# Modulation products in a two-block transformer kernel: held behind weight products in three feed-forwards, begun earlier in the last mixer

## The chip, the cores and the metric

One core of one Trainium2 chip. The metric is the device time of one execution in microseconds, given as the median of three runs.

## The reference

Everything is float32, 256 tokens of width 1024. Block 1 has two layers (mixer, layer norm, a relu-squared feed-forward, a per-layer gate). Block 2 has two layers, each of this form (`mod_c`, `hc` are the same for a context stream of 256 tokens):

```
mod = (silu(c) @ w_mod[i] + b_mod[i])              # 1024 x 6144 weights
sh1, sc1, g1, sh2, sc2, g2 = split(mod, 6)          # parts j = 0 .. 5
h = rms_norm(x, norm_mix[i]) * (1 + sc1) + sh1
y = concat([gla, neighbourhood_attention + na bias, sliding_window_attention]) @ w_out[i]   # inputs: h @ w_in[i]
x = x + g1 * y
h = rms_norm(x, norm_ffn[i]) * (1 + sc2) + sh2
x = x + g2 * ((silu(h @ w_gate[i]) * (h @ w_up[i])) @ w_down[i])
```

Parts 3 and 4 (sh2, sc2) are needed at the start of a layer's feed-forward, part 5 (g2) only at its end. They depend on `c` alone, so they can be computed at any time before.

## The kernel before

**Weight products.** All products with large weights go through one stream (`WeightStream`, L201 on). Each unit of up to 512 KB is loaded by SP into a tile `wr` (4 buffers), cast by ScalarE to its high part `wh` (L214) and split by VectorE into its low part `wl` (L216); TensorE then runs three matmuls per tile and column group (high by high, low by high, high by low), for instance L279 to L281 in the mixers and L1473 to L1475 in the last feed-forwards' gate and up products. DMA issues stand in SP's queue in one order; an issue that waits for a free buffer holds all that follow it.

**Modulations.** `modulation(l, box, js)` (L938) gives four pieces per part j. A piece loads two 512 KB tiles of w_mod (L955) and runs eight matmuls (L957), which the trace shows as 16 records, into a PSUM tile `fil`; VectorE adds the sum to `bm` or `gate` (L959), and after the fourth piece some small work makes the scale and shift `mf`. The w_mod tiles use the tag `fr`, which has 2 buffers. The neighbourhood attention of block 2's layers loads its bias (L1214, one tile for each of three head pairs) into the same two buffers.

**Order.** The kernel's text makes lists of pieces, puts them together with `weave(a, b)` (spreads b evenly over a) and runs them in that order; a scheduler in the framework then places the instructions of each engine by its own estimate of times, so that a piece of the list may move ahead of what stands before it. On the chip each engine works its own queue in that order.

**Last layer's mixer** (block 2 layer 1). 16 pieces of dense input products come first, then further dense pieces and the gated linear attention (GLA, L1053 to L1160 on TensorE). They form `rest` (L1450); the attention pieces (scores L1229, maxima L1239 and L1242, which reads the bias, exponentials L1249, products with values L1285) are woven between. `side["swa"]` holds here the modulations of parts 3 and 4 (eight pieces), woven into the pieces from the sixteenth on. Then comes the output projection (L279 to L281), and between it and the feed-forward the norm with its transposes (L177, tile `sc`, from `a`, L996), the high and low split (L378, L379) and the sums of squares. I call this stretch the seam.

**Feed-forwards with modulations woven in.** Block 1 layer 1 has part 4 of layer 0; block 2 layer 0 has part 2 of layer 1; the last feed-forward has part 5 of layer 1 (four pieces).

## Time and profile before

| | us |
|---|---|
| median of three runs (lowest, highest) | 1923.53 (1917.25, 1923.91) |
| the profiled execution | 1920.0 |
| its span | 1918.2 |
| TensorE busy in it | 1842.1 (96%) |

The span runs from the first to the last instruction that the profiler shows; the profiled execution's own time is 1.8 us longer. Engines: PE is TensorE, DVE is VectorE, ACT is ScalarE, POOL is GpSimd, SP issues DMAs. "L957" is a line of the kernel before. In a timeline row the bracket gives how long the engine sat idle before it, and what it waited for. A clock of 1.00 is 2.4 GHz, and the lower level is 1.2 GHz; a window's figure is the mean over it. Starts of rows that follow each other closely tell TensorE's pace; the length of a single matmul includes its way through the array.

### The profile page before, as it was taken

The numbers are of one execution on the slowest core, as the hardware profiler recorded it, in microseconds if no ns is written. First come the engines' busy times: TensorE is split into PE (matmuls) and PEld (weight loads), VectorE is DVE, ScalarE is ACT, GpSimd is POOL, SyncE is SP. The second block draws the span as 40 slices with busy tenths as digits, with TensorE's granted clock in tenths as the row PEclk, the third lists the DMA queues.
The fourth block names the chain that finished last, engine by engine and source line by source line (L and its number), as shares of the span: only waits on it lengthen the run. The fifth ranks groups of instructions, "written<-read, shape, count | busy, mean of one in ns | idle before, by whom it ended". The sixth has DMA issues, their size and how long they took to land. (4 is left out here: it accounts for less than half of the span.)

```text
span 1918.2 us, 31907 instructions
## 1 busy us (share of the span) xinstructions
PE 1842.1 (96%) x12481; PEld 1574.4 (82%) x12481; DVE 1224.2 (64%) x2333; ACT 988.7 (52%) x1630; POOL 51.0 (3%) x74
## 2 busy tenths in 40 slices
PE   7999999999999899999899999999999999989997
PEld 5766888997887688888787889899898886669997
DVE  5565656656666666668577876685646666755545
ACT  5463564554565364544568553454546556344443
POOL 1000000000000000000000000000000000000000
PEclk9999999999999899999899999999999999989999
DMA  8746654545756554465353355556665464456652
GB/s 282 253 162 212 217 184 144 176 154 192 220 167 198 191 189 151 169 219 174 118 170 103 122 163 167 168 182 192 195 212 168 153 187 146 140 177 187 184 181 98
DMA packets 100835, 338.84 MB, mean 177 GB/s; under 512 B 11572, under 2 KB 12812, under 8 KB 100684
## 3 DMA queue, kind: packets, MB, share of 16 engines
q1 hardware_dynamic: 100140, 336.43, 54.3%
q8 instruction: 98, 1.61, 0.3%
q0 software_dynamic: 544, 0.36, 0.2%
q14 instruction: 53, 0.43, 0.1%
HBM read 335.70 MB, written 1.05 MB: 176 GB/s over the span
## 5 line engine op out<-in xcount | busy, mean ns | idle before, releaser
L216 DVE TENSOR_TENSOR wl<-wr,wh 128x1024 fp32r<-128x1024 f32 (+3 forms) x562 | 638.0, 1137 | 412.6 <-ACT wh L214 406.0
L214 ACT CAST wh<-wr 128x1024 fp32r<-128x1024 f32 (+3 forms) x562 | 549.6, 981 | 655.5 <-PE acc L281 134.6
L279 PE MATMUL acc<-wh,mh 128*128 128x256 f32 (+3 forms) x400 | 132.0, 336 | 3.5 <-ACT mh L378 2.0
L280 PE MATMUL acc<-wl,mh 128*128 128x256 f32 (+3 forms) x400 | 130.8, 329 | 0.7 <-DVE wl L216 0.7
L281 PE MATMUL acc<-wh,ml 128*128 128x256 f32 (+3 forms) x400 | 131.1, 330 | 0.0
L279 PE MATMUL acc<-wh,xh 128*128 128x512 f32 (+3 forms) x304 | 117.0, 394 | 6.1 <-ACT xh L378 3.8
L280 PE MATMUL acc<-wl,xh 128*128 128x512 f32 (+3 forms) x304 | 117.9, 388 | 2.5 <-DVE wl L216 2.5
L281 PE MATMUL acc<-wh,xl 128*128 128x512 f32 (+3 forms) x304 | 117.4, 387 | 0.1
L850 PE MATMUL acc<-wh,a 128*128 128x512 f32 x256 | 102.4, 403 | 0.0
L851 PE MATMUL acc<-wl,a 128*128 128x512 f32 x256 | 101.9, 398 | 0.0
L852 PE MATMUL acc<-wh,a 128*128 128x512 f32 x256 | 101.6, 398 | 0.0
L1473 PE MATMUL sc<-xh,wh 128*128 128x256 f32 x352 | 99.7, 284 | 0.0
L1474 PE MATMUL sc<-xl,wh 128*128 128x256 f32 x352 | 99.5, 283 | 0.0
L1475 PE MATMUL sc<-xh,wl 128*128 128x256 f32 x352 | 99.5, 283 | 0.0
L1474 PE MATMUL sc<-ml,wh 128*128 128x256 f32 x352 | 99.1, 282 | 0.0
L1473 PE MATMUL sc<-mh,wh 128*128 128x256 f32 x352 | 98.9, 281 | 0.0
L1475 PE MATMUL sc<-mh,wl 128*128 128x256 f32 x352 | 98.4, 279 | 0.0
L279 PEld LDWEIGHTS acc<-wh,mh 128*128 128x128 f32 x400 | 75.2, 189 | 14.1 <-issue 3.2
L280 PEld LDWEIGHTS acc<-wl,mh 128*128 128x128 f32 x400 | 75.7, 189 | 6.6 <-DVE wl L216 1.3
L281 PEld LDWEIGHTS acc<-wh,ml 128*128 128x128 f32 x400 | 75.6, 189 | 6.7 <-issue 0.6
L279 PEld LDWEIGHTS acc<-wh,xh 128*128 128x128 f32 x304 | 58.1, 193 | 22.8 <-ACT wh L214 4.6
L825 PE MATMUL sc<-mh,wh 128*128 128x256 f32 x256 | 74.6, 293 | 1.6 <-DVE ml L358 1.6
(570 smaller groups left out, 4683.4 us busy)
## 6 DMA issues: line engine op xcount, KB each, us to landing
wr<-in_ffn_w_dram SPq DMA_DIRECT2D x128, 512.0 KB
fr<-in_w_mod_dram SPq DMA_DIRECT2D x90, 512.0 KB
wr<-in_w_gate_dram SPq DMA_DIRECT2D x66, 512.0 KB
wr<-in_w_up_dram SPq DMA_DIRECT2D x66, 512.0 KB
wr<-in_w_down_dram SPq DMA_DIRECT2D x66, 512.0 KB
wr<-in_w_in_dram SPq DMA_DIRECT2D x40, 384.0 KB
wr<-in_ev_w_in_dram SPq DMA_DIRECT2D x28, 512.0 KB
wr<-in_w_in_dram SPq DMA_DIRECT2D x28, 512.0 KB
```

The source lines that it names most:

```text
L214: S.copy(hi, raw)
L216: V.tensor_tensor(lo, raw, hi, ALU.subtract)
L279: mm(o, xh[:, k, :], wh[:, kk, :], start=(u == 0 and kk == 0), stop=False)
L280: mm(o, xh[:, k, :], wl[:, kk, :], start=False, stop=False)
L281: mm(o, xl[:, k, :], wh[:, kk, :], start=False, stop=(u == nu - 1 and kk == 1))
L825: mm(o, wh[:, kk, bs], mh, start=(k == 0 and b % 2 == 0), stop=False, skip_group_check=True)
L850: mm(o, hh[:, b, ts_], wh[:, kk, :], start=(b == 0), stop=False)
L851: mm(o, hh[:, b, ts_], wl[:, kk, :], start=False, stop=False)
L852: mm(o, hl[:, b, ts_], wh[:, kk, :], start=False, stop=(b == 3))
L1473: mm(o, wh[:, kk, bs], mh, start=(k == 0 and b == 0), stop=False, skip_group_check=True)
L1474: mm(o, wh[:, kk, bs], ml, start=False, stop=False, skip_group_check=True)
L1475: mm(o, wl[:, kk, bs], mh, start=False, stop=(k == 7), skip_group_check=True)
```

## The change

Every third matmul of a weight product goes through a wrapper that remembers it as `dense[0]`. `modulation` takes `hold`; where it is set, a piece's eight matmuls are told to stand behind the last weight product that had been written when the piece was. It is set for the three feed-forwards' modulations. In the last mixer the first four of the eight pieces of parts 3 and 4 are woven into the first 16 dense pieces, and the other four into the rest.

```diff
+    dense = []
+    def wm(*args, **kw):
+        dense[:] = [mm(*args, **kw).ins]
...
-                mm(o, xl[:, k, :], wh[:, kk, :], start=False, stop=(u == nu - 1 and kk == 1))
+                wm(o, xl[:, k, :], wh[:, kk, :], start=False, stop=(u == nu - 1 and kk == 1))
...
-    def modulation(l, box, js):
+    def modulation(l, box, js, hold):
...
-                for g in range(4):
-                    mm(ps[32 * g:32 * g + 32, 0:256], cT[:, k, :], raw[:, 256 * g:256 * g + 256],
-                       start=(k == 2 * u), stop=(k == 2 * u + 1), tile_position=(0, 32 * g))
+                with (tc.issue_after(dense[0]) if hold else nullcontext()):
+                    for g in range(4):
+                        mm(ps[32 * g:32 * g + 32, 0:256], cT[:, k, :], raw[:, 256 * g:256 * g + 256],
+                           start=(k == 2 * u), stop=(k == 2 * u + 1), tile_position=(0, 32 * g))
...
-            rest = dense[:16] + weave(dense[16:] + g, side["swa"])
+            rest = weave(dense[:16], side["swa"][:4]) + weave(dense[16:] + g, side["swa"][4:])
...
-                                                        ffn=weave(ctx_b[:-2], mod(0, 4)), end=flat(ctx_b[-2:]), last=[]))
+                                                        ffn=weave(ctx_b[:-2], mod(0, 4, hold=True)), end=flat(ctx_b[-2:]), last=[]))
...
-        "na": ffn_n, "swa": ffn_c, "pre": [], "from": 2, "ffn": weave([do(layer2_params, 1, prs[1])] + G(["norm", "kv", "znv", "gla"]), mod(1, 2)), "end": L(["nk", "skv"])})
+        "na": ffn_n, "swa": ffn_c, "pre": [], "from": 2, "ffn": weave([do(layer2_params, 1, prs[1])] + G(["norm", "kv", "znv", "gla"]), mod(1, 2, hold=True)), "end": L(["nk", "skv"])})
...
-        "swa": mod(1, 3, 4), "from": 2, "ffn": mod(1, 5), "end": [],
+        "swa": mod(1, 3, 4), "from": 2, "ffn": mod(1, 5, hold=True), "end": [],
```

The instructions move in three places only. In block 1 layer 1's feed-forward one group of four modulation matmuls moves back by 24 rows of TensorE's queue; in block 2 layer 0's nothing moves. The other two places are below; lines from L938 on stand 7 or 8 further down in the changed kernel, and the third matmul of a weight product has the wrapper's line, L157.

TensorE's queue before, where the last mixer's attention and dense products meet: `sc` are scores of one pair of heads and one half of the tokens, `sm` and `acc` its transposed weights, `acc` of L1285 its product with the values, `wh` and `wl` weights.

```order
L1229 MATMUL sc_16127<-a_3091_15894,a_3076_15793 128x256
...
L1229 MATMUL sc_16241<-a_3091_15894,a_3076_15793 128x256
...
L177 MATMUL sm_16147<-ident_61,t_3133_16041 128x128 x4
L177 MATMUL acc_16153<-ident_61,t_3134_16042 128x128 x4
L1285 MATMUL acc_16159<-t_3135_16053,a_3056_15657 64x128
...
L177 MATMUL sm_16261<-ident_61,t_3155_16133 128x128 x4
L279 MATMUL acc_16225<-wh_16069,mh_15310 128x512
L280 MATMUL acc_16225<-wl_16071,mh_15310 128x512
L281 MATMUL acc_16225<-wh_16069,ml_15311 128x512
```

The same place now, up to the same weight products (L286, L287; here `acc_16302`), with the modulation's `fil`:

```order
L1237 MATMUL sc_16127<-a_3091_15894,a_3076_15793 128x256
...
L965 MATMUL fil_16071<-fr_16072,cT_72 32x256 x4
L965 MATMUL fil_16071<-fr_16078,cT_72 32x256 x4
L184 MATMUL sm_16147<-ident_61,t_3133_16041 128x128 x4
L184 MATMUL acc_16153<-ident_61,t_3134_16042 128x128 x4
...
L1237 MATMUL sc_16239<-a_3091_15894,a_3076_15793 128x256
...
L1237 MATMUL sc_16338<-a_3091_15894,a_3076_15793 128x256
...
L184 MATMUL sm_16259<-ident_61,t_3156_16133 128x128 x4
L184 MATMUL acc_16265<-ident_61,t_3157_16134 128x128 x4
L1293 MATMUL acc_16271<-t_3158_16145,a_3056_15657 64x128
...
L286 MATMUL acc_16302<-wh_16087,mh_15310 128x512
```

The dense products now stand behind a piece of modulation, another pair's scores (`sc_16338`) and the whole of the second attention set (`sm_16259` to L1293).

SP's queue before, at the same place; `na_bias` loads are those that the attention's L1242 (now L1250) reads.

```order
L1214 DMA fr_15939<-in_na_bias_dram 128x1024
L1214 DMA fr_16123<-in_na_bias_dram 128x1024
L212 DMA wr_15260<-in_w_in_dram 128x768
...
L212 DMA wr_16284<-in_w_in_dram 128x1024
L1214 DMA fr_16345<-in_na_bias_dram 128x1024
L212 DMA wr_16302<-in_w_in_dram 128x1024
L212 DMA wr_16320<-in_w_in_dram 128x1024
L955 DMA fr_16585<-in_w_mod_dram 128x1024
```

And now:

```order
L1222 DMA fr_15939<-in_na_bias_dram 128x1024
L962 DMA fr_16072<-in_w_mod_dram 128x1024
L219 DMA wr_15260<-in_w_in_dram 128x768
...
L219 DMA wr_16316<-in_w_in_dram 128x1024
L962 DMA fr_16078<-in_w_mod_dram 128x1024
L219 DMA wr_16381<-in_w_in_dram 128x1024
L1222 DMA fr_16123<-in_na_bias_dram 128x1024
L219 DMA wr_16399<-in_w_in_dram 128x1024
L962 DMA fr_16283<-in_w_mod_dram 128x1024
L962 DMA fr_16289<-in_w_mod_dram 128x1024
L1222 DMA fr_16334<-in_na_bias_dram 128x1024
L962 DMA fr_16470<-in_w_mod_dram 128x1024
```

The second pair's bias (`fr_16123`) stood right behind the first pair's before; now a w_mod load has that place, and the bias is issued behind a second w_mod load and a weight load. The third pair's (`fr_16345` before, `fr_16334` now) is issued behind two more w_mod loads.

TensorE's queue in the seam before, between the last output products and the feed-forward; `fil` are pieces of part 5, `sc` the norm's transposes.

```order
L281 MATMUL acc_17389<-wh_17275,c_3095_15900 128x512
L957 MATMUL fil_17918<-fr_17919,cT_72 32x256 x4
L957 MATMUL fil_17918<-fr_17925,cT_72 32x256 x4
L177 MATMUL sc_17365<-ident_61,a_3432_17362 128x128 x4
L177 MATMUL sc_17377<-ident_61,a_3432_17362 128x128 x4
L957 MATMUL fil_18262<-fr_18263,cT_72 32x256 x4
L957 MATMUL fil_18262<-fr_18269,cT_72 32x256 x4
L177 MATMUL sc_17427<-ident_61,a_3442_17424 128x128 x4
L957 MATMUL fil_18606<-fr_18607,cT_72 32x256 x4
L177 MATMUL sc_17439<-ident_61,a_3442_17424 128x128 x4
L957 MATMUL fil_18606<-fr_18613,cT_72 32x256 x4
```

And now:

```order
L157 MATMUL acc_17389<-wh_17275,c_3095_15900 128x512
L184 MATMUL sc_17365<-ident_61,a_3432_17362 128x128 x4
L184 MATMUL sc_17377<-ident_61,a_3432_17362 128x128 x4
L184 MATMUL sc_17427<-ident_61,a_3442_17424 128x128 x4
L184 MATMUL sc_17439<-ident_61,a_3442_17424 128x128 x4
L1481 MATMUL sc_17457<-xh_17185,wh_17305 128x256
L1481 MATMUL sc_17458<-xh_17185,wh_17317 128x256
L1482 MATMUL sc_17457<-xl_17186,wh_17305 128x256
```

Four pieces of part 5 stand now inside the feed-forward, each in one block of eight matmuls; before, three stood in the seam, and the fourth in the feed-forward in two parts, of one and of seven matmuls.

## Rows read from the trace of the kernel before

**Rows 1.** The page, busy time of TensorE: us, share of the span, instructions

```profile
PE 1842.1 (96%) x12481; PEld 1574.4 (82%) x12481; DVE 1224.2 (64%) x2333; ACT 988.7 (52%) x1630; POOL 51.0 (3%) x74
```

**Rows 2.** Windows: start:end, length, busy of each engine, TensorE's clock, DMA share, GB/s

```profile
1632.00:1640.00 8.00, 8.00 (x58) 5.67 (x58) 7.12 (x27) 1.98 (x8) 1.03 (x2) 0.64 0.05 8
1640.00:1672.00 32.00, 27.57 (x319) 19.98 (x316) 24.66 (x91) 12.03 (x39) 1.95 (x3) 1.00 0.56 181
1728.00:1776.00 48.00, 48.00 (x351) 45.57 (x350) 25.63 (x25) 21.94 (x25) 0.00 (x0) 1.00 0.63 190
```

**Rows 3.** Timeline of TensorE, last mixer's start: start, us, operation, [idle before <-releaser]

```profile
1574.80 0.60 PE L1229 MATMUL sc<-ck,a 64*128 64x256 f32 x4
...
1579.39 0.76 PE L177 MATMUL sm<-ident,t 128*128 128x128 f32 x4
...
1582.84 0.81 PE L177 MATMUL sm<-ident,t 128*128 128x128 f32 x4
1583.41 0.48 PE L279 MATMUL acc<-wh,mh 128*128 128x512 f32 x1
```

**Rows 4.** Timeline of SP's DMA issues, last mixer's start

```profile
1573.50 0.40 SPq L1214 DMA_DIRECT2D fr<-in_na_bias_dram  x1
1574.64 2.72 SPq L212 DMA_DIRECT2D wr<-in_w_in_dram  x2
```

**Rows 5.** Timeline of VectorE, last mixer's start

```profile
1576.92 0.48 DVE L1242 CUSTOM_DVE_ANT_0 t<-sc,fr,mx 128x256 f32<-128x256 f32 x1
```

**Rows 6.** Chain of waits, GLA phase: start, length, what

```profile
1659.05 3.82 DMA fr<-in_w_mod_dram
```

**Rows 7.** Chain of waits, seam between last mixer and last feed-forward

```profile
1702.31 6.26 DMA fr<-in_w_mod_dram
```

**Rows 8.** Timeline of TensorE, GLA phase

```profile
1626.39 1.07 PE L957 MATMUL fil<-fr,cT 128*32 128x256 f32 x16 [1.48 <-DVE bm L959]
...
1663.01 0.64 PE L957 MATMUL fil<-fr,cT 128*32 128x256 f32 x8 [3.00 <-DMA fr<-in_w_mod_dram]
```

**Rows 9.** Timeline of TensorE, the seam

```profile
1701.17 1.07 PE L957 MATMUL fil<-fr,cT 128*32 128x256 f32 x16
1704.92 1.09 PE L177 MATMUL sc<-ident,a 128*128 128x128 f32 x8 [2.67 <-DVE a L996]
...
1708.61 1.08 PE L957 MATMUL fil<-fr,cT 128*32 128x256 f32 x8 [1.06 <-DMA fr<-in_w_mod_dram]
1712.29 1.09 PE L177 MATMUL sc<-ident,a 128*128 128x128 f32 x4 [2.59 <-DVE a L996]
...
1716.38 0.38 PE L1473 MATMUL sc<-xh,wh 128*128 128x256 f32 x1
1716.60 0.28 PE L1474 MATMUL sc<-xl,wh 128*128 128x256 f32 x1
1716.71 0.28 PE L1475 MATMUL sc<-xh,wl 128*128 128x256 f32 x1
...
1719.43 0.62 PE L957 MATMUL fil<-fr,cT 128*32 128x256 f32 x2
```

**Rows 10.** Timeline of VectorE, the seam

```profile
1709.76 0.43 DVE L959 TENSOR_TENSOR gate<-fil,gate 128x256 f32<-128x256 f32 x1 [0.74 <-PE fil L957]
```

**Rows 11.** Timeline of TensorE, start of block 1 layer 1's feed-forward

```profile
662.23 0.58 PE L825 MATMUL sc<-mh,wh 128*128 128x256 f32 x1 [1.64 <-DVE ml L358]
662.61 0.41 PE L826 MATMUL sc<-ml,wh 128*128 128x256 f32 x1
662.83 0.41 PE L827 MATMUL sc<-mh,wl 128*128 128x256 f32 x1
...
668.53 0.28 PE L825 MATMUL sc<-mh,wh 128*128 128x256 f32 x1
668.65 0.28 PE L826 MATMUL sc<-ml,wh 128*128 128x256 f32 x1
```

**Rows 12.** Timeline of TensorE, inside the last feed-forward

```profile
1865.57 1.06 PE L957 MATMUL fil<-fr,cT 128*32 128x256 f32 x14
```

More of the change, by code (lines that the diff above doesn't have):

```diff
@@ L1 @@
 import math
+from contextlib import nullcontext
 from contextlib import ExitStack
@@ L326, in part @@
                     mm(o, wh[:, kk, bs], ml, start=False, stop=False, skip_group_check=True)
-                    mm(o, wl[:, kk, bs], mh, start=False, stop=(k == kdim - 1), skip_group_check=True)
+                    wm(o, wl[:, kk, bs], mh, start=False, stop=(k == kdim - 1), skip_group_check=True)
             if 2 * u == kdim - 2:
@@ L826, in up_part @@
                     mm(o, wh[:, kk, bs], ml, start=False, stop=False, skip_group_check=True)
-                    mm(o, wl[:, kk, bs], mh, start=False, stop=(k == 7), skip_group_check=True)
+                    wm(o, wl[:, kk, bs], mh, start=False, stop=(k == 7), skip_group_check=True)
             if u == 3:
@@ L851, in down_part @@
                             mm(o, hh[:, b, ts_], wl[:, kk, :], start=False, stop=False)
-                            mm(o, hl[:, b, ts_], wh[:, kk, :], start=False, stop=(b == 3))
+                            wm(o, hl[:, b, ts_], wh[:, kk, :], start=False, stop=(b == 3))
                     if 1 in hs:
@@ L1474, in up_part @@
                     mm(o, wh[:, kk, bs], ml, start=False, stop=False, skip_group_check=True)
-                    mm(o, wl[:, kk, bs], mh, start=False, stop=(k == 7), skip_group_check=True)
+                    wm(o, wl[:, kk, bs], mh, start=False, stop=(k == 7), skip_group_check=True)
             if m == 1 and u == 1:
@@ L1500, in down_part @@
                             mm(o, hh[:, kk, ts_], wl[:, kk, :], start=False, stop=False)
-                            mm(o, hl[:, kk, ts_], wh[:, kk, :], start=False, stop=(kk == 1 and g == NG - 1))
+                            wm(o, hl[:, kk, ts_], wh[:, kk, :], start=False, stop=(kk == 1 and g == NG - 1))
                     if NG - 1 in gs:
@@ L1553, in up_part @@
                     mm(o, wh[:, kk, bs], ml, start=False, stop=False, skip_group_check=True)
-                    mm(o, wl[:, kk, bs], mh, start=False, stop=(k == 7), skip_group_check=True)
+                    wm(o, wl[:, kk, bs], mh, start=False, stop=(k == 7), skip_group_check=True)
             if u == 0:
@@ L1579, in down_part @@
                         mm(o, h[:, 0, kk, ts_], wl[:, kk, :], start=False, stop=False)
-                        mm(o, h[:, 1, kk, ts_], wh[:, kk, :], start=False, stop=(kk == 1))
+                        wm(o, h[:, 1, kk, ts_], wh[:, kk, :], start=False, stop=(kk == 1))
                     if g == 0:
@@ L1661, in body, with mod @@
     program = [do(begin)]
-    def mod(l, *js):
-        return modulation(l, boxes[l], js)
+    def mod(l, *js, hold=False):
+        return modulation(l, boxes[l], js, hold)
     program += block1_layer(0, xTs[0], to_next(1), dict(tail=flat(ctx_a[:1]), lr=4, mix=mod(0, 0, 1) + ctx_n + mod(0, 2), first=flat(ctx_a[1:2]) + mod(0, 3),
```

## The prediction

> **What bounds the kernel now.** I began with the page: TensorE is busy 96% of the span [rows 1], so the time is its work, plus the stretches where it idles or runs at the low clock. The windows say where those are. In the last feed-forward it has no idle time at all, 48.00 of 48.00 us at full clock [rows 2]: what is put in there costs its whole length. In the last mixer's GLA phase it idles, 4.43 of the 32 us from 1640, and from 1632 to 1640 it works all the time but at a mean clock of 0.64 [rows 2]: VectorE's and ScalarE's chain decides there, and work put between is partly free. The timeline of the seam gives waits of 2.67, 1.06 and 2.59 us, 6.32 in all [rows 9], and the chain of waits passes there through a load of w_mod that took 6.26 us from issue to landing, a piece of the modulation and VectorE's L959 [rows 7, 9, 10]. No modulation matmul disappears: the change moves pieces between these three kinds of stretch.
>
> **The two early holds.** In block 1 layer 1's feed-forward one block of four matmuls goes back by 24 rows, among weight products, and in block 2 layer 0's nothing moves. TensorE meets the same work in both; the bound from both sides is one block's length, half of the 1.07 us that 16 records take [rows 8], and I take 0.
>
> **The seam and the last feed-forward.** Four terms.
> First, the chain loses L959 and what it waits for. Before, VectorE stood 0.74 us and worked 0.43 us on the gate sum at 1709.76 [rows 10], in front of the sums of squares of the second half of the tokens; and between the second half's two sets of transposes, the first of them at 1712.29, stands a piece of 1.08 us [rows 9]. Without these the second half's transposes begin about 1.5 us earlier, and the feed-forward's first product, at 1716.38 before [rows 9], at about 1714.4 (2.0 earlier; 1.5 if the second set of transposes no longer matters, as the split's chain behind the first one then ends last). The last 6.26 us load is no longer on the chain. I take -2.0, bounds -1.2 and -3.0. The 6.32 us can't all be won, since 5.26 of them wait for `a` of the norm itself, which needs no modulation piece.
> Second, the clock. Before, the feed-forward's steps are 0.11 to 0.12 us from its second product on (1716.60 to 1716.71 [rows 9]): pieces and transposes had kept TensorE at work without a gap from 1712.29, 4.1 us at the low clock, and it was up when the first product came. In block 1 layer 1 the feed-forward starts after idle time, without such pieces: its steps are 0.22 us (662.61 to 662.83) from the start at 662.23 and 0.12 us from 668.53 on [rows 11], so some 6.2 us at the low clock (1.2 GHz), of which 45% is lost against the high one. Between 4.1 and 6.2 us I take the seam's own 4.1, so +1.8; bounds 0 (it stays up) and +2.8.
> The Trainium skill, TensorE: Matmul & The Clock Gate, Part 1, has the low clock as the default, released by activity. With that rule the seam without its pieces ends in a cold start; a reading by which only a long pause lowers the clock would leave this term out, and the sum 1.8 us lower. These rows side with the page.
> Third, three pieces go from the seam, where they lay mostly in time that TensorE idled anyway, to a stretch without idle time: 3 x 1.05 = +3.15 (16 records in 1.07 us at the high clock [rows 8, 9], and 14 in 1.06 inside this feed-forward [rows 12]). Nothing hides them, so the bounds are +2.9 and +3.3.
> Fourth, the first matmul of the fourth piece, alone at 1719.43 and in the next product's way until 1719.98 [rows 9], joins its other seven: -0.55.
> Sum: -2.0 + 1.8 + 3.15 - 0.55 = +2.4, bounds -0.6 (-3.0 + 0 + 2.9 - 0.55) and +4.4 (-1.2 + 2.8 + 3.3 - 0.55). The w_mod loads go behind weight loads; with four weight buffers and a window of 1728 to 1776 in which DMA is busy 0.63 of the time [rows 2] I count nothing for it.
>
> **The last mixer's start.** The second head pair's bias was loaded before the mixer began; now it takes the buffer of the first w_mod tile. It can be issued only after that tile's four matmuls, which stand behind the scores that end at 1575.40 [rows 3], so at about 1576.0, and SP comes to it after a weight load of the kind that passed at 1574.64 [rows 4]. The nearest rows for its landing are 3.82 us [rows 6] and 6.26 us [rows 7], so it lands between 1579.8 and 1582.3. VectorE's L1242, which reads it, ran at 1576.92 [rows 5]; behind it in VectorE's queue wait the low parts of weights and the rotary work, so VectorE as a whole stands 2.9 to 5.4 us. From that L1242 to the second set's transposes were 5.92 us (1582.84 [rows 3]), so these come between 1585.7 and 1588.2; the transposes and value products of the first set took 3.45 us from 1579.39 to 1582.84 [rows 3], and the second set's now stand whole before the dense products, which begin between 1589.2 and 1591.7 instead of 1583.41: 5.8 to 8.3 us late. Work that came later is done by then: a modulation piece 1.07, one more set's scores 1.1 (twice the four of [rows 3]), the second set's remaining part about 1.5 at the high clock (half of 3.45 less the transposes that stood there anyway), six rotary transposes some 0.9 (four in 0.76 [rows 3]); together about 4.6. Net +1.2 to +3.7; I take +2.5.
> For this load the Trainium skill, DMA: Bandwidth & Descriptors, Anatomy of one DMA, gives a fixed 2.0 us and 436 GB/s for the GpSimd path, so an estimate of 3.2 us for 512 KB. By it the start would be late by 0.6 us less, and the sum lower by as much; both rows are longer, and I stay with them.
> The third pair's bias waits in the same way behind two w_mod loads. By then TensorE has dense products with four split weights ahead, which cover a stand of VectorE of that size; 0 here, and up to 3.8 us [rows 6] if the cover is used up.
>
> **The GLA phase.** It keeps four of its eight pieces, and one attention set fewer: 4 x 1.07 + about 1.9 (a little over half of the 3.45 us at the low clock) = 6.2 us less for TensorE. In the dense part these 6.2 us cost in full. In the GLA phase they give back between nothing (VectorE's chain alone sets the pace) and all (they stand in the way), and beyond that the 3.00 us wait for w_mod and the 1.48 us wait for L959 [rows 8], since the two `fr` buffers are asked for half as often. Between these ends, a loss of 6.2 and a gain of 4.5, I take half the fillers and half the waits: +3.1 - 2.2, rounded +1. The phase idles already, 4.43 in 32 [rows 2], and this is the row nearest to a chain that sets the pace; the gain from the waits is seen in the rows as well. This is the widest term.
> Mixer: +2.5 + 1 = +3.5, bounds -3.3 and +13.7 (3.7 + 3.8 + 6.2).
>
> **Sum.** 0 + 2.4 + 3.5 = about +6 on the profiled execution's 1920.0. The three timed runs lie from 1917.25 to 1923.91, and their median is 3.5 us above the profiled one; the mean of the four is 1921.2. I add 6 to that: 1927.
>
> **Rivals.**
> *The waits go and nothing replaces them.* The GLA phase loses all its 4.43 us of idle time, the 3.00 among them, the 1.48, and the cold stretch from 1632 to 1640 (0.36 of 8 us, 2.9 [rows 2]); the bias comes in time at the mixer's start; and the seam gives its 2.0 with the clock staying up, so that the last feed-forward loses only 0.6. Together -8.8 + 0.6, some -8: 1913. For it: those waits are in the rows. Against it: the bias can't be issued before its buffer is free.
> *The bias decides.* Its load is issued late and takes the 6.26 us; the third bias stalls VectorE again by 3.8 when the split weights are used up; the GLA phase, without fillers, is paced by VectorE and ScalarE and gives nothing back. Mixer 3.7 + 3.8 + 6.2 = 13.7, seam at 3.5: +17, 1938. It decides from the point where the bias lands later than about 1582. For it: one in-order queue for SP, two buffers. Against it: the 27.57 of 32 us that TensorE is busy in the phase [rows 2], so that pieces do stand in its way.
> *It does not show.* The pieces only change places: what the mixer loses at its start it gains in its GLA phase, and what the feed-forward takes over, the seam gives. Within 2 us of 1921. For it: no work goes away. Against it: the feed-forward has no idle time at all.
>
> **How the numbers follow.** Forecast 0.40, waits go 0.18, bias decides 0.24, does not show 0.18. Half a per cent, about what a measurement can tell from no change, is 9.6 us on the median: faster is under 1913.9, slower over 1933.1. Of the first rival 0.11 lies under 1913.9, with 0.06 from the lower edges of the forecast and the last rival: 0.17 faster. Of the second 0.19 lies above 1933.1, with 0.07 from the forecast's upper edge: 0.26 slower. The rest, 0.57, is the same. The forecast's own range is 1920 to 1934; that which leaves 2 in 10 out is 1912 to 1940.
>
> **What would show it.** In the profile after: the feed-forward's first product 2 us sooner behind the last output product than the 15 us of before (1701.17 to 1716.38 [rows 9]), steps of 0.22 us for some 4 us behind it, and four blocks of 16 records inside the feed-forward. At the mixer's start, L1250 of the second pair waiting for `na_bias`, and dense products some 7 us later behind the first scores than before. In the GLA phase, fewer waits for w_mod, more for VectorE and ScalarE. If the bias lands before L1250 is reached, the mixer's start is wrong; if the feed-forward starts with steps of 0.12 us, the clock term is; if TensorE's idle share in the GLA phase falls, the first rival is right.

## The result and the profile after

The changed kernel takes 1936.28 us (median of four runs, 1935.70 to 1937.65) against 1923.37 before (median of four too): a ratio of 1.0081, 95% interval 1.0057 to 1.0106, so 0.8% slower. The profiled execution took 1936.37 us, its span is 1934.6. I had said 1927, with 1920 to 1934 as the forecast's own range and 1912 to 1940 as the wide one. The time is 9 us above the forecast, outside the first range and inside the second, over the 1933.1 from which I called it slower (a chance of 0.26), and nearest to the rival in which the bias decides (1938).

The line of the page that answers to [rows 1]:

```profile
PE 1851.9 (96%) x12481; PEld 1583.7 (82%) x12481; DVE 1224.6 (63%) x2333; ACT 989.5 (51%) x1630; POOL 51.3 (3%) x74
```

TensorE was busy 9.8 us longer with the same 12481 matmuls, so a part of the loss is slower matmuls, not idle time alone.

Executions of either kernel reach block 1 layer 1's feed-forward at different times (651 to 660 us in the profiles of this study), so I compare stretches. From the transposes in front of that feed-forward to those in front of the last mixer it is 874 us in both kernels (653.20 to 1527.45 before, 652.85 to 1526.76 after): the two early holds cost nothing that shows. All the loss lies behind 1527, where it is 17 us. By stretches:

| stretch | before | after | difference | forecast |
|---|---|---|---|---|
| second pair's first scores to the dense products | 9.14 | 17.38 | +8.2 | +5.8 to +8.3 |
| dense products, to their last (1615.12; 1624.41) | 31.71 | 33.31 | +1.6 | |
| from there to the output projection | 61.38 | 65.49 | +4.1 | about -5 |
| output projection | 24.36 | 23.06 | -1.3 | |
| seam | 15.52 | 13.92 | -1.6 | -2.0 |
| last feed-forward to the end of the span | 201.82 | 207.72 | +5.9 | +4.4 |

The sum is +16.9, and the scores stood 0.55 us earlier: 16.4, the difference of the spans. ("About -5" is the +1 of the GLA phase's term without the 6.2 us of work that it left to the stretches ahead of it.) The -1.3 of the output projection is work that moved: four matmuls each of L975 and L992 (L967 and L984 before) stand in the stretch ahead of it now, so of the +4.1 there 1.3 are theirs.

**The mixer's start.** Timeline of TensorE in the changed kernel, to be read beside [rows 3]:

```profile
1573.72 0.71 PE L1237 MATMUL sc<-a,a 64*128 64x256 f32 x4
...
1575.04 0.64 PE L965 MATMUL fil<-fr,cT 128*32 128x256 f32 x8 [0.17 <-ACT skT L1304]
1577.44 0.64 PE L965 MATMUL fil<-fr,cT 128*32 128x256 f32 x8 [1.76 <-DMA fr<-in_w_mod_dram]
...
1581.21 0.89 PE L1237 MATMUL sc<-a,a 64*128 64x256 f32 x3 [1.09 <-DVE mx L1250]
...
1585.13 1.62 PE L1237 MATMUL sc<-a,a 64*128 64x256 f32 x4 [0.93 <-DVE mx L1250]
...
1591.10 0.50 PE L286 MATMUL acc<-wh,mh 128*128 128x512 f32 x1
```

The dense products begin at 1591.10, in the forecast's 1589.2 to 1591.7. The second w_mod tile holds TensorE 1.76 us, and two sets of scores wait for the maxima (`mx`, L1250) 1.09 and 0.93 us. Before, one such wait was all:

```profile
1577.46 0.70 PE L1229 MATMUL sc<-a,a 64*128 64x256 f32 x2 [2.05 <-DVE mx L1242]
```

SP's issues there, beside [rows 4] (w_mod, weight, bias):

```profile
1572.94 0.40 SPq L962 DMA_DIRECT2D fr<-in_w_mod_dram  x1
1574.08 0.33 SPq L219 DMA_DIRECT2D wr<-in_w_in_dram  x1
1575.73 0.33 SPq L1222 DMA_DIRECT2D fr<-in_na_bias_dram  x1
```

And VectorE's first L1250 that needs this bias, beside [rows 5]:

```profile
1580.67 0.48 DVE L1250 CUSTOM_DVE_ANT_0 t<-sc,fr,mx 128x256 f32<-128x256 f32 x1
```

The bias went out at 1575.73, behind a w_mod tile and a weight, and L1250, at 1576.92 before, ran at 1580.67. It is not marked as waiting: the new order had put the rotary work and the modulation's L967 ahead of it, so VectorE worked while the bias came, with waits of 0.35 and 0.57 us for TensorE. The trace's semaphore records have the bias landing at 1580.64, 4.9 us after its issue, between the 3.82 and 6.26 us of the rows that I had gone by. So the bias and VectorE's own new order reached 1580.67 together, and this trace doesn't say which of them alone would have held L1250.

**The GLA phase.** Windows of scores to dense products, of the dense products, and from there to the output projection, before (length, busy TensorE, weight loads, VectorE, ScalarE, GpSimd, then TensorE's clock, DMA share and GB/s):

```profile
1574.27:1583.41 9.14, 7.09 (x45) 5.40 (x45) 6.71 (x23) 5.68 (x14) 0.00 (x0) 0.81 0.62 224
1583.41:1615.45 32.04, 32.04 (x189) 24.52 (x187) 22.10 (x61) 19.41 (x34) 0.00 (x0) 1.00 0.41 132
1615.45:1676.50 61.05, 53.43 (x562) 37.87 (x561) 45.45 (x158) 30.49 (x78) 4.13 (x6) 0.94 0.45 148
```

And after:

```profile
1573.72:1591.10 17.38, 12.85 (x96) 8.97 (x95) 13.18 (x47) 8.77 (x21) 0.00 (x0) 0.80 0.56 210
1591.10:1624.73 33.63, 33.63 (x218) 24.95 (x216) 20.54 (x56) 18.54 (x34) 0.00 (x0) 1.00 0.50 172
1624.73:1689.90 65.17, 56.61 (x489) 41.73 (x489) 41.54 (x144) 28.86 (x71) 4.00 (x6) 0.84 0.30 98
```

The first lines take the mixer's start apart: of the 8.2 us, 2.5 are idle time of TensorE (4.53 against 2.05) and 5.8 busy time, 51 matmul records more. The 9.14 us are this profile's own: in three others with the same order there the stretch is 7.69 us, with the same 45 or 46 records at the full clock, as in the kernel with the holds alone:

```profile
1580.78:1588.47 7.69, 5.57 (x45) 4.17 (x45) 5.30 (x19) 5.44 (x14) 0.00 (x0) 1.00 0.74 268
```

The third line is the surprise: the phase has three modulation pieces and one attention set less in it, and yet is longer. Its idle time rose by 0.9 us only (7.62 to 8.56), but the mean clock fell from 0.94 to 0.84. Length times the missing share of the clock is 3.7 us before and 10.4 after. The stretch comes again in other profiles: 61.07 and 61.08 us in two with the mixer of before, 65.43 in one with the changed mixer. Its tail, first one row of before, then the changed kernel:

```profile
1670.30 2.00 PE L1151 MATMUL acc<-a,t 128*128 128x64 f32 x16
```

```profile
1660.17 0.63 PE L965 MATMUL fil<-fr,cT 128*32 128x256 f32 x4
...
1676.45 1.29 PE L1125 MATMUL acc<-t,t 64*128 64x128 f32 x16 [2.19 <-DVE t L1118]
1679.29 1.94 PE L1159 MATMUL acc<-a,t 128*128 128x64 f32 x8 [1.56 <-DVE t L1129]
...
1682.21 1.97 PE L1159 MATMUL acc<-a,t 128*128 128x64 f32 x8
```

The last piece of modulation starts at 1660.17. In the 30 us behind it, TensorE waits 2.19 and 1.56 us for VectorE, and the value products (L1159, L1151 before) run at the low clock: sixteen took 2.00 us in one row before, here eight take 1.94 to 1.97. One of the eight pieces now lies in front of the dense products and two among them, where TensorE has no idle time to fill, and the tail has none.

**The seam and the last feed-forward**, beside [rows 9, 11]:

```profile
1712.96 0.39 PE L157 MATMUL acc<-wh,c 128*128 128x512 f32 x1
1716.92 1.97 PE L184 MATMUL sc<-ident,a 128*128 128x128 f32 x8 [3.58 <-DVE a L1004]
1723.43 1.94 PE L184 MATMUL sc<-ident,a 128*128 128x128 f32 x8 [4.54 <-DVE a L1004]
1726.88 0.80 PE L1481 MATMUL sc<-xh,wh 128*128 128x256 f32 x2 [1.51 <-ACT xh L385]
...
1728.22 0.41 PE L1481 MATMUL sc<-xh,wh 128*128 128x256 f32 x1
1728.44 0.41 PE L1482 MATMUL sc<-xl,wh 128*128 128x256 f32 x1
...
1733.50 0.28 PE L1482 MATMUL sc<-xl,wh 128*128 128x256 f32 x1
1733.62 0.28 PE L157 MATMUL sc<-xh,wl 128*128 128x256 f32 x1
```

L959 and the pieces are gone, and the first product follows the last output product by 13.92 us instead of 15.52. The steps are then 0.21 to 0.22 us until 1733.50, 6.6 us at the low clock where I took 4.1 (how far one profile tells this is said below). The first eight transposes, too, take 1.97 us, where [rows 9] have 1.09. The four pieces inside look like this one, and cost 1.07 us each:

```profile
1846.62 1.07 PE L965 MATMUL fil<-fr,cT 128*32 128x256 f32 x16
```

### The profile page after: what moved, and what is told of

It is laid out like the page before. It is cut to its first block, busy times and chain, and to the rows that moved or that the text cites. A ratio compares the mean times of both kernels' runs of the same rounds, so it can differ in the third digit from the quotient of the medians.

```text
span 1934.6 us, 31900 instructions
## 1 busy us (share of the span) xinstructions
PE 1851.9 (96%) x12481; PEld 1583.7 (82%) x12481; DVE 1224.6 (63%) x2333; ACT 989.5 (51%) x1630; POOL 51.3 (3%) x74
## 5 line engine op out<-in xcount | busy, mean ns | idle before, releaser
L157 PE MATMUL acc<-wh,a 128*128 128x512 f32 x472 | 186.9, 397 | 0.0
L157 PE MATMUL sc<-xh,wl 128*128 128x256 f32 x608 | 173.2, 285 | 0.0
L157 PE MATMUL sc<-mh,wl 128*128 128x256 f32 x608 | 170.6, 281 | 0.0
L286 PE MATMUL acc<-wh,mh 128*128 128x256 f32 (+3 forms) x400 | 132.2, 336 | 3.5 <-ACT mh L385 2.0
L287 PE MATMUL acc<-wl,mh 128*128 128x256 f32 (+3 forms) x400 | 130.5, 328 | 0.7 <-DVE wl L223 0.7
L157 PE MATMUL acc<-wh,ml 128*128 128x256 f32 (+3 forms) x400 | 131.0, 329 | 0.0
L286 PE MATMUL acc<-wh,xh 128*128 128x512 f32 (+3 forms) x304 | 117.7, 397 | 5.8 <-ACT xh L385 3.8
L287 PE MATMUL acc<-wl,xh 128*128 128x512 f32 (+3 forms) x304 | 118.3, 389 | 2.1 <-DVE wl L223 2.1
L157 PEld LDWEIGHTS sc<-xh,wl 128*128 128x128 f32 x608 | 117.7, 194 | 0.2
L157 PE MATMUL acc<-wh,xl 128*128 128x512 f32 (+3 forms) x304 | 117.7, 388 | 0.1
L157 PEld LDWEIGHTS sc<-mh,wl 128*128 128x128 f32 x608 | 114.8, 189 | 1.0 <-issue 1.0
L157 PEld LDWEIGHTS acc<-wh,a 128*128 128x128 f32 x472 | 89.1, 189 | 21.5
L857 PE MATMUL acc<-wh,a 128*128 128x512 f32 x256 | 102.0, 402 | 0.0
L1481 PE MATMUL sc<-mh,wh 128*128 128x256 f32 x352 | 98.9, 281 | 0.0
L286 PEld LDWEIGHTS acc<-wh,mh 128*128 128x128 f32 x400 | 75.2, 189 | 14.3 <-issue 3.0
L157 PEld LDWEIGHTS acc<-wh,ml 128*128 128x128 f32 x400 | 75.5, 189 | 7.1 <-issue 1.0
```

What stands on the lines that cost most here:

```text
L157: dense[:] = [mm(*args, **kw).ins]
L286: mm(o, xh[:, k, :], wh[:, kk, :], start=(u == 0 and kk == 0), stop=False)
L287: mm(o, xh[:, k, :], wl[:, kk, :], start=False, stop=False)
L857: mm(o, hh[:, b, ts_], wh[:, kk, :], start=(b == 0), stop=False)
L1481: mm(o, wh[:, kk, bs], mh, start=(k == 0 and b == 0), stop=False, skip_group_check=True)
```

## Experiments

All ran beside the kernel before; the ratios are to its runs on the same chip, with a 95% interval. Edits show the changed parts of their lines, and `...` stands for what is left out.

**One edit at a time.** The mixer's list alone:

```diff
-ffn=weave(ctx_b[:-2], mod(0, 4, hold=True))
+ffn=weave(ctx_b[:-2], mod(0, 4))
...
-mod(1, 2, hold=True)), "end": L(["nk", "skv"])})
+mod(1, 2)), "end": L(["nk", "skv"])})
...
-"ffn": mod(1, 5, hold=True), "end": [],
+"ffn": mod(1, 5), "end": [],
```

> The changed kernel without the three holds: only the last mixer's edit. If the two edits add up, the mixer alone gives what its stretch shows in the profile of the changed kernel (the output projection ends 12.1 us later, 1712.96 against 1700.86), and the seam and the last feed-forward are as before: about 1921 + 12 = 1933 us. If the mixer's loss is made good in the seam, or comes in part from the holds (the scheduler plans all together), under 1929. If the holds cost nothing, 1936.

1934.78 us, ratio 1.0068 (1.0050 to 1.0086). The mixer's edit alone gives nearly the whole loss. But the stretches differ from what I expected: its seam isn't as before, it is 20.62 us long, since the scheduler put all four pieces of part 5 into it. Timeline of TensorE there:

```profile
1710.15 1.06 PE L965 MATMUL fil<-fr,cT 128*32 128x256 f32 x14
...
1716.01 1.08 PE L965 MATMUL fil<-fr,cT 128*32 128x256 f32 x8 [1.01 <-DMA fr<-in_w_mod_dram]
1717.39 1.08 PE L965 MATMUL fil<-fr,cT 128*32 128x256 f32 x8 [0.31 <-DMA fr<-in_w_mod_dram]
1721.79 2.30 PE L965 MATMUL fil<-fr,cT 128*32 128x256 f32 x16 [3.32 <-DMA fr<-in_w_mod_dram]
...
1728.28 0.64 PE L965 MATMUL fil<-fr,cT 128*32 128x256 f32 x8 [2.45 <-DVE xl L386]
1729.44 1.08 PE L965 MATMUL fil<-fr,cT 128*32 128x256 f32 x8 [0.52 <-DMA fr<-in_w_mod_dram]
```

Behind the first, the pieces wait for their w_mod loads (1.01, 0.31, 3.32 and 0.52 us) and once for VectorE (2.45). In exchange its feed-forward takes 202.45 us to the end of the span, though it too starts at the low clock (5.4 us), and the stretch from the dense products to the output projection 62.62 instead of 65.49, with the same pieces in it. So with the mixer's new list the holds save 6.7 us in the seam and 0.7 in the output projection, and pay 5.3 in the feed-forward and 2.9 in the GLA phase: a cost of 0.6 us from the last mixer's transposes to the end, 1.5 between the medians, whose intervals overlap. The two edits don't simply add.

The holds alone:

```diff
-            rest = weave(dense[:16], side["swa"][:4]) + weave(dense[16:] + g, side["swa"][4:])
+            rest = dense[:16] + weave(dense[16:] + g, side["swa"])
```

> The changed kernel with the last mixer's list as before: only the holds. My sum of the seam and the feed-forward was +2.4; the profile of the changed kernel shows 1.6 us less from the last output product to the first feed-forward product and 5.9 us more from there to the end, +4.3. Expected 1925 us, with some 6 us of steps of 0.21 us at the feed-forward's start. Rival: the low clock there comes from the mixer's edit, then the feed-forward starts at the high clock and the time is 1922 or less.

1920.81 us, ratio 1.0001 (0.9985 to 1.0018). Its seam is 13.65 us, its feed-forward 206.73 to the end, together 3.0 more than before, with 4.3 us at the low clock: the low clock doesn't come from the mixer's edit. The time doesn't show the 3 us; the interval goes from -2.9 to +3.5, so it allows them and as well nothing. The cost of the holds alone is read from these stretches, not shown by the time.

**The bias in its own buffers**, on the changed kernel:

```diff
-                    nbt[0] = T([P, 2, 2, 256], F32, "fr", 2)
+                    nbt[0] = T([P, 2, 2, 256], F32, "bc" if l else "fr", 2)
```

> The changed kernel with the last layer's attention bias in two other buffers, so that w_mod tiles no longer stand before it. Theory (the bias's wait is what delays the dense products): they begin at about 1586 to 1587 instead of 1591.10, the GLA phase with its first matmul L1061 as much earlier, and the time is 4 to 5 us less, about 1932 us. Rival (the pieces and sets placed in front of the dense products are the delay, the bias lies beside it): they begin at 1590 or later, time 1935 to 1936 us.

1928.97 us, ratio 1.0040 (1.0027 to 1.0054): 7.3 us less than the changed kernel, more than expected. TensorE at the mixer's start:

```profile
1572.77 0.71 PE L1237 MATMUL sc<-a,a 64*128 64x256 f32 x4
...
1574.08 1.07 PE L965 MATMUL fil<-fr,cT 128*32 128x256 f32 x16 [0.17 <-ACT skT L1304]
...
1583.87 0.50 PE L286 MATMUL acc<-wh,mh 128*128 128x512 f32 x1
```

The stretch as a window:

```profile
1572.77:1583.87 11.10, 10.10 (x82) 7.28 (x81) 8.08 (x28) 5.68 (x14) 0.00 (x0) 0.85 0.77 281
```

It is 11.10 us instead of 17.38, but not with the same work in it: 82 matmul records instead of 96, as the third pair's scores and six rotary transposes stay behind here. Of the 6.3 us, 3.5 are idle time (1.00 against 4.53) and 2.8 busy time, and the dense products take 35.42 us instead of 33.31; at their end 4.2 us of the gain are left. So the bias behind w_mod costs about 4 us ahead of the GLA phase, its wait and the order made for it together. The GLA phase is shorter too, from L1061 to the output projection 57.78 us instead of 60.51, at a clock of 0.88 (0.83 in the changed kernel, shown below):

```profile
1624.27:1682.05 57.78, 49.61 (x442) 36.52 (x441) 37.86 (x136) 26.48 (x67) 4.01 (x6) 0.88 0.29 96
```

**The GLA phase.** First the decays ahead of the dense products' end, on the kernel before:

```diff
-            rest = dense[:16] + weave(dense[16:] + g, side["swa"])
+            rest = dense[:12] + g[:1] + dense[12:16] + weave(dense[16:] + g[1:], side["swa"])
```

> The kernel before, with the GLA's decays (L1053 and its exponentials and logarithms) put after the twelfth of the 16 dense pieces instead of behind them. In both profiles the stretch from that matmul to the output projection is the same, 61.05 us before and 60.51 after, whatever pieces lie in it. Theory (a chain over ScalarE and VectorE from there paces the phase): the phase behind the dense products gets shorter by 3 to 6 us, the time is about 1916 to 1919 us. Rival (TensorE's own work, its waits for w_mod and the low clock set the phase): no change, 1921 us, or more, as VectorE gets late with the weights' low parts.

1920.74 us, ratio 1.0001 (0.9986 to 1.0015). L1053 ran at 1603.57, 17.7 us before the dense products' end, and the phase behind them was 58.85 us instead of 61.38; but the dense stretch grew by 3.2. My theory, a chain from L1053 that paces the phase, isn't borne out: the phase gives 2.5 us instead of 3 to 6, and the dense products take them back.

The pieces taken out of the mixer, on the kernel before:

```diff
-mod(1, 2)), "end": L(["nk", "skv"])})
+mod(1, 2, 3, 4)), "end": L(["nk", "skv"])})
...
-        "swa": mod(1, 3, 4), "from": 2, "ffn": mod(1, 5), "end": [],
+        "swa": [], "from": 2, "ffn": mod(1, 5), "end": [],
```

> The kernel before, with the eight modulation pieces of parts 3 and 4 moved out of the last mixer into the feed-forward of the layer before (where they cost some 8 x 1.05 = 8.4 us). It asks what the pieces are worth in the GLA phase, from L1053 to the output projection, 61.05 us before with all eight in it (8.6 us of matmuls). Theory (ScalarE and VectorE pace the phase, and pieces only fill waits): still 57 to 60 us, with a lower mean clock than 0.94; time 1925 to 1930. Rival (the pieces stand in TensorE's way, as half of them did in my sum): 52 to 54 us, time 1921 or less.

1950.44 us, ratio 1.0149 (1.0131 to 1.0167), far over both. The dense products that begin at 1583.41 before begin at 1609.60, and 22 us of that lie ahead of the mixer: the 874 us up to its transposes are 896.3 here, where I had counted 8.4 for the eight pieces. Attention sets moved at the mixer's start too, so the total says nothing on my question. The phase itself, from L1053 to the output projection:

```profile
1650.03:1704.10 54.07, 40.70 (x338) 32.06 (x337) 33.61 (x113) 24.28 (x61) 3.35 (x6) 0.81 0.03 11
```

54.07 us, at the edge of the rival's 52 to 54 and 3 below the theory's 57: the 8.6 us of pieces bought 7.0 us of time, while TensorE's busy time fell by 12.7 us and the mean clock to 0.81. Inconclusive as a price of pieces, since sets moved too; but the low clock comes with missing pieces here as well.

Then blocks of matmuls in the changed kernel's phase that do nothing but keep TensorE at work:

```diff
+    def filler(n, ins):
+        for _ in range(n):
+            ps = PT("fil")
+            with tc.issue_after(ins):
+                for k in range(2):
+                    for g in range(4):
+                        mm(ps[32 * g:32 * g + 32, 0:256], cT[:, k, :], C("causal"), start=(k == 0), stop=(k == 1), tile_position=(0, 32 * g))
...
+            if wset and not e.ctx:
+                filler(1, lasttr[0])
```

One block stands behind each half's transposes, as shown, and one behind each half's scores.

> The changed kernel with four extra blocks of 16 matmul records in the last GLA, one behind each half's transposes and one behind each half's scores; their results are used by nothing. Theory (the phase lost its pieces, idles in their place, and so runs at the low clock from 1676 to 1689): the mean clock from L1061 to the output projection rises from 0.84 to 0.90 or more, the 60.51 us become 57 to 58, the time about 1933. Rival (the chain over ScalarE and VectorE sets the pace whatever the clock): 60.5 us or up to 4 more, 1936 to 1940.

1933.02 us, ratio 1.0063 (1.0041 to 1.0084), 3.3 less than the changed kernel. The two intervals overlap, so the stretches have to tell. TensorE in the tail (L194 are the blocks, L1138 and L1174 what L1125 and L1159 are in the changed kernel):

```profile
1675.57 1.07 PE L194 MATMUL fil<-cst,cT 128*32 128x256 f32 x16
1676.89 1.79 PE L1138 MATMUL acc<-t,t 64*128 64x128 f32 x16 [0.25 <-DVE t L1131]
1678.61 1.07 PE L194 MATMUL fil<-cst,cT 128*32 128x256 f32 x16
1679.77 1.07 PE L976 MATMUL fil<-fr,cT 128*32 128x256 f32 x16
1680.77 1.10 PE L1174 MATMUL acc<-a,t 128*128 128x64 f32 x8
```

The waits of 2.19 and 1.56 us have become 0.25 and 0, and eight of L1174 take 1.10 us instead of 1.94. But not by the blocks alone: the row at 1679.77 is a piece of modulation. The scheduler put two of the pieces back into the tail (from 1667.62 and 1679.77; in the changed kernel the last begins at 1660.17), and TensorE waits 5.00 us for `mx` at 1646.04. The tail from the transposes in front of L1125 (here L1138) to the output projection, in the changed kernel and in this one:

```profile
1673.66:1689.90 16.24, 12.49 (x109) 11.10 (x108) 9.24 (x31) 3.69 (x15) 2.59 (x4) 0.68 0.00 1
1674.98:1688.52 13.54, 13.20 (x167) 9.74 (x165) 10.03 (x36) 4.50 (x22) 2.96 (x4) 1.00 0.24 80
```

2.7 us less, with 58 matmul records more in it, at the full clock. The window from L1061 to the output projection in the changed kernel:

```profile
1629.39:1689.90 60.51, 51.95 (x441) 38.80 (x441) 38.11 (x136) 26.48 (x67) 4.00 (x6) 0.83 0.28 92
```

And in this one:

```profile
1632.71:1688.52 55.81, 49.27 (x506) 35.47 (x505) 38.55 (x136) 26.36 (x67) 4.00 (x6) 0.94 0.30 100
```

4.7 us less, with four blocks more in it, at 0.94 instead of 0.83. That speaks against a pace set by ScalarE and VectorE whatever the clock: with the waits filled, by blocks and by pieces, the same chain was done sooner. It doesn't price the missing pieces alone. The kernel with the mixer's edit only has the same number of pieces from L1061 on and 442 records to the changed kernel's 441, and takes 57.64 us there, at 0.88: the order that comes with the holds has a part in the low clock too.

**The seam**, with such blocks on the changed kernel, three of them between the halves' transposes:

```diff
+                if l == 1:
+                    filler(1, last_wm[0])
                 rms_mod(x[t], xT2["T"], t, 0, box["mf"], 3, a4, ms)
+                if l == 1:
+                    filler((2, 0)[t], lasttr[0])
```

> The changed kernel with extra blocks of 16 matmul records in the seam, three of them between the two halves' transposes; their results are used by nothing. Theory (the start of the feed-forward runs at the low clock because the seam has no pieces; 6.6 us of steps of 0.21 us): fewer than 2.5 us of such steps, from the first product to the end 205 us instead of 207.7, the seam not longer than 14.5. Rival (the blocks delay the second half's transposes by as much as the clock gives): seam 16 or more, the two stretches together 221 us or more as now. Time about 1933 against 1936.

1938.47 us, ratio 1.0093 (1.0076 to 1.0110). TensorE in the seam (48 records of blocks in the second row):

```profile
1720.46 1.09 PE L187 MATMUL sc<-ident,a 128*128 128x128 f32 x8 [2.17 <-DVE a L1016]
1721.48 3.39 PE L195 MATMUL fil<-cst,cT 128*32 128x256 f32 x48
...
1726.55 1.73 PE L187 MATMUL sc<-ident,a 128*128 128x128 f32 x8 [1.68 <-DVE a L1016]
```

The blocks didn't delay the transposes. The first eight took 1.09 us instead of 1.97, the seam 11.90 instead of 13.92, the low clock at the feed-forward's start lasted 3.9 us instead of 6.6, and from there to the end it is 206.50 instead of 207.72. One block fell into the output projection, which took 1.27 us more, so that it and the seam together won 0.8 us. In all 2.0 us less; the total is not less, and 2 us are below what it tells. The theory isn't shown: I had expected less than 2.5 us at the low clock and 2.7 us less in the feed-forward, and 3.9 us is little below the 4.3 to 6.6 us that five profiles without such blocks have.

**Both mixer costs at once**: the bias in its own buffers and the blocks in the GLA.

```diff
-                    nbt[0] = T([P, 2, 2, 256], F32, "fr", 2)
+                    nbt[0] = T([P, 2, 2, 256], F32, "bc" if l else "fr", 2)
...
+            if wset and not e.ctx:
+                filler(1, lasttr[0])
```

> The changed kernel with both of the mixer's suspected costs taken away at once: the bias in its own two buffers, and the four extra blocks of matmul records in the GLA. If the bias's wait and the low clock are two separate costs, their gains add: dense products 11 us behind the first scores instead of 17.4, the stretch from L1061 to the output projection about 56 us at a mean clock of 0.94, time 1936.3 - 7.3 - 3.3 = about 1926 us. If they are one cost (the late start is what empties the phase's tail; with the bias alone the phase is 57.8 us already), the second adds nothing to the first: 1929 us. What is left above the kernel before, about 4 to 6 us, would be the pieces in the last feed-forward and its cold start.

1925.89 us, ratio 1.0026 (1.0010 to 1.0041). The time is what the sum of both gains gives. From L1061 to the output projection:

```profile
1622.27:1678.75 56.48, 50.13 (x506) 36.14 (x505) 38.67 (x136) 26.30 (x67) 4.01 (x6) 0.91 0.29 99
```

With the bias alone it is 57.78, with the blocks alone 55.81: in this stretch the two gains overlap, and the blocks add 1.3 us to the bias's gain instead of 4.7. Another 1.1 us lies at the mixer's start, 9.97 us from the first scores to the dense products instead of 11.10, with the same 82 records, but at a clock of 1.00 instead of 0.85: the blocks stand elsewhere, and this is no gain of theirs. So the total fits the sum (its interval overlaps with that of the bias alone), but the two costs are not separate: with the bias in time the phase's clock was up at 0.88 without any block. From the last mixer's transposes to the end of the span this kernel takes 398.1 us, the changed one 407.8, the one before 390.7: of 17.1 us, 9.7 go with the two edits. Of the 7.4 that remain, 3.9 are the seam and the feed-forward (13.92 + 207.29 against 15.52 + 201.82). The other 3.5 lie in the mixer: 3.7 in the dense products (35.42 against 31.71), which have pieces and sets among them that lay elsewhere before, 0.8 at the mixer's start, and -1.3 in the output projection.

**Two new versions.** The GLA over the dense products, on the kernel before:

```diff
-            rest = dense[:16] + weave(dense[16:] + g, side["swa"])
-            prog += weave(rest, att[:-1], True) + [do(rows)] + weave(att[-1:], outp[:1])
+            prog += weave(dense[8:16] + weave(dense[:8], g[:4]), att[:6], True)
+            prog += weave(weave(g[4:], side["swa"]), att[6:-1], True) + [do(rows)] + weave(att[-1:], outp[:1])
```

> A new version of the kernel before: in the last mixer the dense products that the GLA needs come first, and the GLA's first four pieces are woven into the other eight dense pieces, the sliding-window sets behind them. The phase behind the dense products has 7.6 us of idle time and 3.7 us of low clock before; if dense products fill them, 5 to 10 us are gained, 1911 to 1916 us. Rival (VectorE, 45 of 61 us busy there, is what the phase and the weights' low parts both wait for): no gain, 1919 to 1925.

1941.79 us, ratio 1.0105 (1.0089 to 1.0121), far over both. L1053 starts at 1592.10, but from the dense products to the output projection it is 69.0 us instead of 61.4, 10.0 of them idle instead of 7.6. The sliding-window sets stand all behind the dense products, as before, and a neighbourhood set with them. What makes the difference was not taken apart.

The bias in its own buffers on the kernel before (the edit shown above):

> A new version of the kernel before: only the attention bias of the last layer in its own two buffers, no other change; the order of TensorE's queue stays. The first two w_mod tiles are then loaded a hundred us earlier, and the others wait only for each other. If the two shared buffers hold the GLA phase up (3.00 us of wait for w_mod and 1.48 for L959 before), 2 to 4 us are gained, 1917; if those waits come from the pieces' own two buffers and one PSUM tile, nothing changes, 1920.

1918.21 us, ratio 0.9997 (0.9978 to 1.0015): no change, though the interval alone would leave room for the 2 to 4 us. The stretches don't: from the dense products to the output projection it is 61.08 us, and the waits for L959 and w_mod are there as before, 1.48 and 2.91 us. The kernel before loaded the bias in time and doesn't need the buffers. No version beat it.

For all kernels, the time from the last mixer's transposes to the end of the span, one profile each:

| kernel | us |
|---|---|
| before; decays early; bias in its own buffers on it | 390.7; 391.0; 389.0 |
| holds alone | 392.2 |
| changed; mixer alone | 407.8; 407.2 |
| changed, bias in its own buffers | 400.6 |
| changed, blocks in the GLA; in the seam | 402.1; 405.9 |
| changed, bias and blocks in the GLA | 398.1 |
| pieces taken out of the mixer (22 us more ahead of it) | 396.6 |
| GLA over the dense products | 408.6 |

## Why the prediction was right, and where it was not

- *Early holds, 0.* Right: the 874 us in which they lie are the same in both.
- *The mixer's start, 5.8 to 8.3 us late.* Right in size against the profile that I read, 8.2; against the 7.69 us of three others it is 9.7, above the range. The bias behind w_mod in two shared buffers is the larger part of the cause: with its own buffers 6.3 us of it go, of which the dense products take 2.1 back. The form is not the one I gave. VectorE didn't stand for 2.9 to 5.4 us, it filled the time with later work, and the sign that I named, L1250 waiting for `na_bias`, isn't in the profile. The cost shows at TensorE: 2.5 us more idle time, as in my +2.5, and 5.8 of work that came earlier, where I had 4.6.
- *The third bias, covered.* Right: TensorE had no idle time in the dense stretch (33.63 of 33.63 us).
- *The GLA phase, +1 with the 6.2 us of work taken ahead of it.* Wrong, and this is the step that failed: "Between these ends ... I take half the fillers and half the waits". I forecast about -5 for the stretch, and it is +4.1 (+2.8 with the output projection, from which 1.3 us of work moved). I priced the pieces as work and as waits for buffers, and not as what keeps the clock up, though I had just priced that in the seam. With three pieces and an attention set less, and a later start, the mean clock went from 0.94 to 0.84; with the waits filled again it was 0.94, and 4.7 us went. What each of the three does to the clock was not separated. Of the waits, that for w_mod did go (3.00 to 0.52 us), but the one for the sum, L959 and now L967, grew from 1.48 to 2.15, as one PSUM tile `fil` serves all pieces:

```profile
1639.89 1.28 PE L965 MATMUL fil<-fr,cT 128*32 128x256 f32 x16 [2.15 <-DVE bm L967]
```

- *The seam -2.0, the pieces +3.15, the first matmul -0.55.* Right: the seam is 1.6 us shorter, and the feed-forward has four whole pieces of 1.07 us. The second half's transposes come 1.0 us earlier behind the last output product, not 1.5: the 0.74 and 0.43 us of [rows 10] make 1.2.
- *The cold start, +1.8.* The mechanism was right: in five profiles with this seam (the changed kernel and those with the holds alone, the bias, the GLA's blocks, and both) the low clock lasts 4.3 to 6.6 us, in three with the seam of before 0.2 to 1.2. The size is not fixed: 6.6 us are 2.9 us of loss, 4.3 are 1.9. Nor would the row of block 1 layer 1 have told it: the same start that took 6.2 us at the low clock there took 3.2 in the changed kernel's profile. The terms of the seam and the feed-forward make +4.3 for +2.4, in my bounds of -0.6 to +4.4.
- *Rivals.* "The bias decides" came nearest in time, 1938 for 1936.28, and in good part by luck. Its condition, a bias that lands later than about 1582, wasn't met (1580.64); the third bias didn't stall TensorE in the dense products; and the phase gave nothing back, but with the clock in it, not by a chain over VectorE and ScalarE alone. "The waits go" was wrong: 1.76, 1.09 and 0.93 us of new waits at the start. "It does not show" was wrong in the mixer.
- *The total.* No error hid another: the GLA phase, the cold start and the mixer's start all came out above what I took, and it is the wide range, 28 us, that still holds the time.

By the Trainium skill, TensorE: Matmul & The Clock Gate, Part 1, activity releases the low clock. The stretch that became 4.7 us shorter with 4.3 us of useless blocks added to it agrees with that.

## What to carry to other kernels

A matmul that fills a wait can be worth more than the time it takes: where the fillers were gone here, matmuls behind the wait ran at half the clock. So count the low clock for every stretch that loses its fillers, not only at the place where the change aims, and read how long it lasts from several profiles. A buffer pool shared between a prefetched tile and a stream of others is a schedule: before moving the stream forward, look in the DMA queue at what stood in the pool first. And compare stretches between two fixed points of the work where executions differ by more than the effect, but count the matmuls in both: a scheduler that plans anew for each edit also moves work across the points.

## What was not expected of the hardware

The stay at the low clock differs between executions of the same code: at the last feed-forward's start 4.3 to 6.6 us in five profiles with the same seam, at block 1 layer 1's 2.9 to 6.3 us in ten, and the mixer's start of before took 7.69 us in three profiles and 9.14, at a clock of 0.81, in one. In the seam, eight transposes behind the same wait of 3.58 us took 1.97 us in one execution and 1.69 in another. Executions of the same code differed by up to 8 us before 660 us, and by less than 1 us over the next 874.
